# Subtracting the mean shift on VectorE instead of by TensorE products, in the last matrix of a layer's feed-forward

## The chip, the cores and the metric

The kernel runs on one core of a Trainium2 chip. The metric is the device time of one execution in microseconds (us); the time before is the median of 3 runs. The core's engines work side by side and wait for each other by semaphores: TensorE (PE in the profile, PEld for its weight loads) multiplies matrices into eight banks of accumulators (PSUM); VectorE (DVE) and ScalarE (ACT) work elementwise; GpSimd (POOL) does little here; SyncE (SP) issues transfers.

## The reference

A trunk of two layers over 256 tokens with 2048 features. Layer 0 mixes by trailing means, layer 1 by dilated attention over a shared K and V; each is followed by a gated feed-forward with a causal convolution of width 3 (inner width 5504). Every block ends in a residual with ALPHA = sqrt(2) and a layer norm:

```python
    for i in range(DEPTH):
        ...
        h = layer_norm(DEEPNORM_ALPHA * h + mix, ln1_g[i], ln1_b[i])
        ff = conv_ffn(h, ffn_w_up[i], ffn_conv_w[i], ffn_conv_b[i], ffn_w_down[i])
        h = layer_norm(DEEPNORM_ALPHA * h + ff, ln2_g[i], ln2_b[i])

def layer_norm(x, g, b):
    mu = jnp.mean(xf, axis=-1, keepdims=True)
    var = jnp.mean(jnp.square(xf - mu), axis=-1, keepdims=True)
    y = (xf - mu) * lax.rsqrt(var + LN_EPS) * g.astype(jnp.float32) + b.astype(jnp.float32)
```

The change lies in the second norm of layer 0. The result of this norm doesn't depend on a constant that is subtracted from all features of a token.

## The kernel before

**Tiling.** Features lie on partitions: the residual is four tiles `H[0]` to `H[3]` ("quarters") of 128 partitions x 4 blocks x 256 tokens. All weights are read as float32 and used as the sum of two parts: ScalarE copies a part of less precision, `wh` (L82), and VectorE takes the difference, `wl` (L83). Each matrix is worked off in units. A unit is a block of up to 512 x 512 weights: it is loaded into one of 3 buffers `raw`, split into one of 4 pairs `wh`, `wl`, and multiplied by an activation tile that is split in the same way. The list `units` sets the order on TensorE; loads run up to 5 units ahead and splits 3. The activations are `xc` (normalized), `xp` (the residual times the norm's gain, not yet normalized) or `g` (gated).

**Order.** Nothing reorders the work: each engine's instructions stand in the order in which the program issues them. A function given to `later(n, fn)` is issued after the products of the n-th unit from there, so its VectorE and ScalarE instructions stand in those queues between the splits of units ahead.

**The matrix in question.** The last three row blocks of the first feed-forward's down matrix (512, 512 and 384 rows) are multiplied by `add_last`, in four groups, one for each quarter of the output, each with four banks. The order of the units is a0 a1 b0 a2 b1 b2 c0 c1 c2 d0 d1 d2, where the letter is the quarter (0 to 3) and the digit the row block. When a group ends, `resid_last` adds its banks to the quarter (L320, L322). The rest is the layer norm:

- After quarter 0, `fold` sums its blocks; one unit later `shift` lets TensorE spread that sum over the partitions (L364), and ScalarE copies it as `cs` (L366). This is a rough mean of each token, subtracted so that the sums of squares keep their precision.
- Quarter 0 has `cs` subtracted by VectorE (L372). Quarters 1 to 3 get it on TensorE: with `shifted`, each bank's last product is followed by one with `neg1`, a constant block whose first row is -1 (L172).
- `stats` squares a quarter on ScalarE (L341) and folds it and its squares into running sums S and Q (L345, L347, L350). `xp` splits the quarter times the gain (L394, L395).
- `chain`, after the first unit of the next matrix, spreads S and Q by two products (L401, L402), works out the factor and the mean (L406 to L410), and then normalizes the quarters one by one (L415, L416, L422, L424; the lower part `xc` by L286).

The next matrix, the shared K weights, starts on `xp`, which needs no statistics (four units over 258 columns); the matrix after it, the queries', needs `xc`. In the first norm of each layer (`first`) the mix has other scalings: there VectorE does the subtraction of quarters 1 to 3 together with the factor ALPHA (L384).

Of the kernel before, what the change touches and what calls it, by code (L numbers as in the profile page):

```python
# [9 lines left out]
F32 = mybir.dt.float32  # L10
F32R = mybir.dt.float32r
I32 = mybir.dt.int32
AF = mybir.ActivationFunctionType
OP = mybir.AluOpType
# [3 lines left out]
T = 256  # L18
P = 128
# [13 lines left out]
def trunk(ctx: ExitStack, tc: tile.TileContext, x, pool_w_in, pool_w_grp, pool_scale, pool_w_out,  # L33
# [3 lines left out]
    V, A, PE = nc.vector, nc.scalar, nc.tensor  # L37
    ctx.enter_context(tc.manual_schedule())

    const = ctx.enter_context(tc.tile_pool(name="const", bufs=1))  # L40
# [7 lines left out]
    def bank(nm):  # L48
        return psp.tile([P, 512], F32, name=nm, tag="ps")
# [12 lines left out]
    def do_load(i, part=None):  # L62
        src = units[i][0]
        if src is None:
            return
        nk, n = src.shape[0] // P, src.shape[1]
        if not part:
            raw[i] = rawp.tile([P, nk, n], F32, name=f"raw{i}", tag="raw")
        rows = src.rearrange("(k p) n -> p k n", p=P)
        ks = pieces(i, nk)  # L70
        for s in ks if part is None else ks[1:] if part else ks[:1]:
            nc.sync.dma_start(raw[i][:, s], rows[:, s])
# [47 lines left out]
    def later(n, fn):  # L120
        if n == 0:
            fn()
        else:
            pending.append([n, fn])
# [22 lines left out]

    XW = T + 2

    def mm_quad(xq, ps, first, last, mode, mid, shifted):  # L150
        def go(h, l):
            nk, nb = h.shape[1], h.shape[2] // P
            order = [(k, m) for k in range(nk) for m in range(nb)]
            if last:
                order = [(k, m) for m in range(nb) for k in range(nk)]
            if first:
                for m in range(nb):
                    ps.append(bank("acc"))
            q = xq()
            n = XW if mode == "x" else T  # L160
            for i, (k, m) in enumerate(order):
                c = slice(m * P, (m + 1) * P)
                st, sp = first and k == 0, last and k == nk - 1
                if mode == "ab":
                    PE.matmul(ps[m], h[:, k, c], q[:, k, :, :T], start=st, stop=False)  # L165
                    PE.matmul(ps[m][:, :T], l[:, k, c], q[:, k, 0, :T], start=False, stop=sp and not shifted)  # L166
                else:
                    PE.matmul(ps[m][:, :n], h[:, k, c], q[:, k, 0, :n], start=st, stop=False)  # L168
                    PE.matmul(ps[m][:, :n], h[:, k, c], q[:, k, 1, :n], start=False, stop=False)  # L169
                    PE.matmul(ps[m][:, :n], l[:, k, c], q[:, k, 0, :n], start=False, stop=sp and not shifted)  # L170
                if sp and shifted:
                    PE.matmul(ps[m][:, :T], neg1, ST["cs"], start=False, stop=True)  # L172
                if mid is not None and i == 7:
                    mid()
        return go

    def group(w, r0s, c0, ncol, xqs, post, mode="ab", mids=(), shifted=False):
        ps = []
        for j, (r0, nr) in enumerate(r0s):
            last = j == len(r0s) - 1  # L180
            units.append((w[r0:r0 + nr, c0:c0 + ncol],
                          mm_quad(xqs[j], ps, j == 0, last, mode, mids[j] if j < len(mids) else None, shifted),
                          (lambda: post(ps)) if last else None))


# [110 lines left out]
    H, XC, XP, ST = {}, {}, {}, {}  # L296
    vec, cvec, gbx = [], [], {}
    ident = const.tile([P, P], F32, name="ident")
    onesd = const.tile([P, P], F32, name="onesd")
    neg1 = const.tile([P, P], F32R, name="neg1")  # L300
    ones4 = const.tile([P, P], F32R, name="ones4")
    epst = const.tile([P, 1], F32, name="epst")
    inv = const.tile([P, 1, 16], F32, name="inv")
# [9 lines left out]
    def resid_last(c, first, lay, which, after):  # L313
        def post(ps):
            for m in range(4):
                y = H[c][:, m, :]
                if first and c == 0:
                    V.scalar_tensor_tensor(y, y, ALPHA, ps[m][:, :T], op0=OP.mult, op1=OP.add)
                else:
                    V.tensor_tensor(y, y, ps[m][:, :T], OP.add)  # L320
                if c < 3:
                    V.tensor_tensor(y, y, ps[m][:, T:], OP.add)  # L322
                if c == 3 and m % 2 == 1:
                    square(3, m - 1)
            if c == 0:
                s = fold(H[0], None, "S0", F32R)
                later(1, lambda: shift(s, first, lay, which))
            elif c < 3:
                n = 3 if c == 1 and not first else 1
                later(n, lambda: stats(c))  # L330
                later(n + 1, lambda: xp(c, lay, which))
            else:
                folds(3)
                xp(3, lay, which)
                later(1, lambda: chain(ps[0], lay, which, after))
        return post
# [20 lines left out]
    def stats(q):  # L357
        square(q, 0)
        square(q, 2)
        folds(q)  # L360

    def shift(s, first, lay, which):
        ps = bank("shift")
        PE.matmul(ps[:, :T], ones4, s, start=True, stop=True)  # L364
        cs = lnp.tile([P, T], F32R, name="cs", tag="cs")
        A.copy(cs, ps[:, :T])  # L366
        ST["cs"] = cs
        cb = cs.bitcast(F32).unsqueeze(1).to_broadcast([P, 4, T])
        ST["S"] = ST["Q"] = None

        def one():
            V.tensor_tensor(H[0], H[0], cb, OP.subtract)  # L372
            if first:
                pre(1)
            stats(0)

        def two():
            xp(0, lay, which)
            if first:
                pre(2)  # L380
                pre(3)

        def pre(q):
            V.scalar_tensor_tensor(H[q], H[q], ALPHA, cb, op0=OP.mult, op1=OP.subtract)  # L384

        later(1, one)
        later(2, two)

    def xp(q, lay, which):
        g0 = 32 * which  # L390
        XP[q] = t = quad_tile("xp")
        for m in range(4):
            g = vec[lay][:, g0 + 4 * q + m:g0 + 4 * q + m + 1]
            A.activation(t[:, m, 0, :T], H[q][:, m, :], AF.Copy, scale=g)  # L394
            V.scalar_tensor_tensor(t[:, m, 1, :T], H[q][:, m, :], g, t[:, m, 0, :T].bitcast(F32),  # L395
                                   op0=OP.mult, op1=OP.subtract)
        A.copy(t[:, :, :, T:], gbx[lay, which][:, 4 * q:4 * q + 4].bitcast(F32))
# [60 lines left out]
    def add_last(w, rows, srcs, first, lay, which, after=None):  # L458
        for c in range(4):
            group(w, rows, 512 * c, 512, srcs, resid_last(c, first, lay, which, after),  # L460
                  mode="a" if c == 3 else "ab", shifted=c > 0 and not first)


    PADW = 16
# [63 lines left out]
    def add_grp(g):  # L528
# [12 lines left out]
             True, 0, 0, after=lambda q: to_tokens(q))  # L541
# [401 lines left out]
    scale = 1.0 / math.sqrt(P)  # L943
# [174 lines left out]
    with tc.tile_pool(name="start", bufs=1) as stp:  # L1118
        one1 = stp.tile([P, P], F32, name="one1")
        for q in range(NQ):  # L1120
            for t in range(2):
                XIN[q, t] = stp.tile([P, 512], F32, name=f"xin{q}{t}")
            halves = [slice(0, 256), slice(256, 512)] if q == 0 else [slice(0, 512)]
            for i, h in enumerate(halves):
                for t in range(2):
                    nc.sync.dma_start(XIN[q, t][:, h], x[0, t * P:(t + 1) * P, 512 * q:512 * q + 512][:, h])
                if q == 0:
                    do_load(0, i)
            if q in (1, 2):
                do_load(q)  # L1130
            if q < 3:
                state["loaded"] = q + 1
            if q == 0:
                make_identity(nc, ident)
                V.memset(one1, 1.0)

                warm = bank("warm")
                for i in range(WARM):
                    PE.matmul(warm[:, :P], one1, one1, start=True, stop=True)
        V.memset(onesd, 1.0 / D)  # L1140
        V.memset(neg1.bitcast(F32), 0.0)
        A.activation(neg1[0:1, :], one1[0:1, :], AF.Copy, scale=-1.0)
        A.activation(ones4, one1, AF.Copy, scale=4.0 / D)
        V.memset(epst, EPS)
        for c in range(16):
            nc.gpsimd.memset(inv[:, :, c:c + 1], 1.0 / (c + 1))
        x_quad(0, (0,))
        warm = bank("warm")
        for i in range(WARM2):
            PE.matmul(warm[:, :P], one1, one1, start=True, stop=True)  # L1150

        run_units(3)
    with tc.tile_pool(name="pool", bufs=1) as pp:
# [5 lines left out]
        for l in range(2):  # L1159
            n = 80 if l == 0 else 64  # L1160
# [95 lines left out]
```

## Time and profile before

| | |
|---|---|
| median of 3 runs | 2023.47 us (2023.33 to 2025.87) |
| the profiled execution | 2024.13 us, its span 2022.0 us |
| granted TensorE clock | 1.000 |
| the stage around the change | some 891 to 970 us from the span's start |

The span goes from the first to the last instruction; the rest lies around it. A row of a timeline gives start and duration in us, engine, line, operation, what it writes and reads, the tile, and how often; in square brackets how long the engine was idle before it and what ended that. TensorE's products overlap: one is listed with 0.28 us, while the next one starts 0.12 us later. A row of stretches gives busy time and instructions of each engine, then the granted clock (1.00 is full speed), the share of the transfer engines and their rate. A row of one line gives the shortest, median and longest duration in ns and the first and last start; rows below it name who ended its waits, with us in total and the number of times.

### The profile page before, as it was taken

What the parts mean: (1) busy time and instruction counts of PE and PEld (TensorE: products, weight loads), DVE (VectorE), ACT (ScalarE), POOL (GpSimd) and SP (SyncE); (2) the same over time, 40 slices, a digit from 0 to 9 for tenths busy, and PEclk for the clock granted to TensorE, in tenths of its full rate; (3) what the DMA queues carried; (4) which work ended last, traced back from release to release, by engine and by line L of the source; (5) the groups of instructions that cost most, each with busy time, mean ns of one, the idle gap of its engine ahead of it and who ended that gap; (6) DMA issues with size and microseconds to landing.
All of it is one profiled execution on the core that took longest, in us unless ns stands there. A gap on an engine that the chain in (4) does not pass through costs nothing.

```text
span 2022.0 us, 31645 instructions
## 1 busy us (share of the span) xinstructions
PE 2014.2 (100%) x12610; PEld 1809.2 (89%) x12610; DVE 1719.5 (85%) x2075; ACT 1270.1 (63%) x1708; POOL 111.3 (6%) x175
## 2 busy tenths in 40 slices
PE   9999999999999999999999999999999999999999
PEld 8898988899889988889898988998899989989987
DVE  6859887899789999889887878787889888989898
ACT  6544686667766686656544544487666676667672
POOL 2000000000000001100001021000001000100100
PEclk9999999999999999999999999999999999999999
DMA  8665477666666758875555656557666756666765
GB/s 259 208 205 187 164 208 211 189 190 224 215 184 192 239 178 228 219 228 179 178 194 174 214 166 205 182 187 215 184 208 190 225 186 219 198 213 194 210 214 181
DMA packets 273699, 406.73 MB, mean 201 GB/s; under 512 B 74782, under 2 KB 91060, under 8 KB 273296
## 3 DMA queue, kind: packets, MB, share of 16 engines
q1 hardware_dynamic: 259488, 388.93, 59.5%
q0 software_dynamic: 13632, 15.13, 5.0%
q8 instruction: 99, 1.62, 0.3%
q10 hardware_dynamic: 432, 0.66, 0.1%
q14 instruction: 48, 0.39, 0.1%
HBM read 380.01 MB, written 2.10 MB: 189 GB/s over the span
## 4 chain that ended last, share of the span: by engine, by line
PE 99%; DMA 0%; SPq 0%; DVE 0%; ACT 0%; issue 0%; DVEq 0%
PE acc L165 44%; PE acc L166 22%; PE s L228 3%; PE s L227 3%; PE s L229 3%; PE acc L169 3%; PE acc L170 3%; PE acc L168 3%; PE t L238 3%; PE t L240 3%; PE t L239 3%; PE t L228 2%; PE t L227 2%; PE t L229 2%; PE s L1040 0%; PE o L1093 0%
## 5 line engine op out<-in xcount | busy, mean ns | idle before, releaser
L165 PE MATMUL acc<-xc,wh 128*128 128x512 f32 x3264 | 1152.0, 396 | 0.0
L166 PE MATMUL acc<-xc,wl 128*128 128x256 f32 x3264 | 916.9, 281 | 0.0
L83 DVE TENSOR_TENSOR wl<-raw,wh 128x2048 fp32r<-128x2048 f32 (+2 forms) x313 | 676.0, 2165 | 207.8 <-ACT wh L82 206.4
L165 PEld LDWEIGHTS acc<-xc,wh 128*128 128x128 f32 x3264 | 616.2, 189 | 143.5 <-issue 0.3
L82 ACT CAST wh<-raw 128x2048 fp32r<-128x2048 f32 (+2 forms) x313 | 564.8, 1810 | 201.7 <-PE acc L165 92.2
L166 PEld LDWEIGHTS acc<-xc,wl 128*128 128x128 f32 x3264 | 615.5, 189 | 0.8 <-DVE wl L83 0.3
L96 ACT CAST wh<-raw 128x1024 fp32r<-128x1024 f32 x126 | 131.7, 1053 | 170.9 <-DVE raw L107 135.5
L97 DVE TENSOR_TENSOR wl<-raw,wh 128x1024 fp32r<-128x1024 f32 x126 | 150.4, 1221 | 3.5 <-ACT wh L96 3.5
L103 ACT CAST wh<-raw 128x1024 fp32r<-128x1024 f32 x126 | 98.7, 834 | 47.8 <-PE acc L165 24.6
L106 DVE TENSOR_TENSOR wl<-raw,wh 128x1024 fp32r<-128x1024 f32 x126 | 114.7, 951 | 4.2 <-ACT wh L103 4.0
L586 ACT ACTIVATE c<-u,cv 128x256 f32<-128x256 f32 x172 | 89.6, 593 | 19.6 <-DVE f L649 8.1
L271 POOL DMA_DIRECT2D ht<-w x24 | 20.4, 850 | 1435.3 <-DVE ht L853 388.1
L228 PE MATMUL t<-wl,g 128*128 128x256 f32 x328 | 92.3, 281 | 0.0
L227 PE MATMUL t<-wh,g 128*128 128x256 f32 x328 | 92.1, 281 | 0.0
L229 PE MATMUL t<-wh,g 128*128 128x256 f32 x328 | 91.9, 280 | 0.0
L577 ACT COPY u<-acc 128x256 f32<-128x256 f32 x164 | 53.8, 372 | 45.9 <-PE acc L166 45.9
L229 PE MATMUL s<-wh,xs 128*128 128x256 f32 x296 | 82.6, 279 | 0.0
L227 PE MATMUL s<-wh,xs 128*128 128x256 f32 x296 | 82.6, 279 | 0.0
L228 PE MATMUL s<-wl,xs 128*128 128x256 f32 x296 | 82.6, 279 | 0.0
L591 ACT ACTIVATE a<-u,cv 128x256 f32<-128x256 f32 x172 | 73.5, 499 | 12.3 <-DVE g L659 6.5
L109 DVE TENSOR_TENSOR raw<-raw 128x1024 f32<-128x1024 f32 x63 | 77.2, 1225 | 2.1
L591 ACT ACTIVATE u<-u,cv 128x256 f32<-128x256 f32 x172 | 73.5, 500 | 0.0
(337 smaller groups left out, 3540.3 us busy)
## 6 DMA issues: line engine op xcount, KB each, us to landing
raw<-in_ffn_w_up_dram SPq DMA_DIRECT2D x160, 1024.0 KB, 5.1
raw<-in_ffn_w_down_dram SPq DMA_DIRECT2D x80, 1024.0 KB, 5.2
raw<-in_pool_w_out_dram SPq DMA_DIRECT2D x16, 1024.0 KB, 5.0
raw<-in_shared_w_k_dram SPq DMA_DIRECT2D x16, 1024.0 KB, 5.3
raw<-in_attn_w_q_dram SPq DMA_DIRECT2D x16, 1024.0 KB, 5.4
raw<-in_shared_w_v_dram SPq DMA_DIRECT2D x16, 1024.0 KB, 5.3
raw<-in_attn_w_o_dram SPq DMA_DIRECT2D x16, 1024.0 KB, 5.3
raw<-in_pool_w_in_dram SPq DMA_DIRECT2D x12, 1024.0 KB, 5.6
```

The lines of the kernel that those rows point to most:

```text
L82: A.copy(wh[i][:, s], r[:, s])
L83: V.tensor_tensor(wl[i][:, s], r[:, s], wh[i][:, s].bitcast(F32), OP.subtract)
L96: A.copy(h[:, :, n], r[:, :, n])
L97: V.tensor_tensor(l[:, :, n], r[:, :, n], h[:, :, n].bitcast(F32), OP.subtract)
L103: A.copy(h[:, k, n], r[:, k, n])
L106: V.tensor_tensor(l[:, k, n], r[:, k, n], h[:, k, n].bitcast(F32), OP.subtract)
L165: PE.matmul(ps[m], h[:, k, c], q[:, k, :, :T], start=st, stop=False)
L166: PE.matmul(ps[m][:, :T], l[:, k, c], q[:, k, 0, :T], start=False, stop=sp and not shifted)
L227: PE.matmul(to, xh, h[:, k, n], start=opens and kk == 0, stop=False)
L228: PE.matmul(to, xh, l[:, k, n], start=False, stop=False)
L229: PE.matmul(to, xl, h[:, k, n], start=False, stop=ends and kk == 1)
L591: A.activation(to[:, m, :], u[:, m, i:i + T], AF.Copy, scale=cv[:, i, j:j + 1])
```

## The change

The twelve products with `neg1` go, with the constant, its fill on VectorE and the activation on ScalarE that sets its first row. In their place VectorE subtracts `cs` from quarters 1, 2 and 3 of the residual, in one instruction over 128 x 1024 each, two, three and four units after `shift`. In the first norms nothing changes.

```diff
-    def mm_quad(xq, ps, first, last, mode, mid, shifted):
+    def mm_quad(xq, ps, first, last, mode, mid):
...
-                    PE.matmul(ps[m][:, :T], l[:, k, c], q[:, k, 0, :T], start=False, stop=sp and not shifted)
+                    PE.matmul(ps[m][:, :T], l[:, k, c], q[:, k, 0, :T], start=False, stop=sp)
...
-                if sp and shifted:
-                    PE.matmul(ps[m][:, :T], neg1, ST["cs"], start=False, stop=True)
...
-    neg1 = const.tile([P, P], F32R, name="neg1")
...
+        def less(q):
+            V.tensor_tensor(H[q], H[q], cb, OP.subtract)
+
         later(1, one)
         later(2, two)
+        if not first:
+            for q in (1, 2, 3):
+                later(1 + q, lambda q=q: less(q))
...
-                  mode="a" if c == 3 else "ab", shifted=c > 0 and not first)
+                  mode="a" if c == 3 else "ab")
...
-        V.memset(neg1.bitcast(F32), 0.0)
-        A.activation(neg1[0:1, :], one1[0:1, :], AF.Copy, scale=-1.0)
```

On VectorE, between the end of quarter 1's residual and the sums of its statistics, these instructions stood before (`wl` are the weight splits of the units d0, d1 and d2, `xp` the split of quarter 0, `fold` and `S` the sums over quarter 1; the lines of the changed program have other numbers):

```order
L322 TENSOR_TENSOR h<-h,acc 128x256
L83 TENSOR_TENSOR wl_8761<-raw_8662,wh_8760 128x2048
L395 SCALAR_TENSOR_TENSOR xp<-h,vec_579,xp 128x256 x4
L83 TENSOR_TENSOR wl_8813<-raw_8704,wh_8812 128x2048
L83 TENSOR_TENSOR wl_8851<-raw_8758,wh_8850 128x1536
L345 TENSOR_TENSOR fold_8885<-h 128x512
L347 TENSOR_TENSOR S<-fold_8885 128x256
```

and these stand there now:

```order
L319 TENSOR_TENSOR h<-h,acc 128x256
L83 TENSOR_TENSOR wl_8754<-raw_8659,wh_8753 128x2048
L398 SCALAR_TENSOR_TENSOR xp<-h,vec_576,xp 128x256 x4
L384 TENSOR_TENSOR h<-h,cs 128x1024
L83 TENSOR_TENSOR wl_8807<-raw_8701,wh_8806 128x2048
L384 TENSOR_TENSOR h<-h,cs 128x1024
L83 TENSOR_TENSOR wl_8846<-raw_8751,wh_8845 128x1536
L384 TENSOR_TENSOR h<-h,cs 128x1024
L342 TENSOR_TENSOR fold_8877<-h 128x512
L344 TENSOR_TENSOR S<-fold_8877 128x256
```

The three subtractions (quarters 1, 2, 3 in this order) stand around the splits of d1 and d2; behind them the queue is the same as before. On TensorE, at the end of the last group, a product with the constant stood between the last product of the unit d2 and the first of the next matrix:

```order
L168 MATMUL acc<-g,wh_8850 128x256
L169 MATMUL acc<-g,wh_8850 128x256
L170 MATMUL acc<-g,wl_8851 128x256
L172 MATMUL acc<-cs,neg_80 128x256
L168 MATMUL acc<-xp,wh_8905 128x258
```

and now the one follows the other:

```order
L168 MATMUL acc<-g,wh_8845 128x256
L169 MATMUL acc<-g,wh_8845 128x256
L170 MATMUL acc<-g,wl_8846 128x256
L168 MATMUL acc<-xp,wh_8897 128x258
L169 MATMUL acc<-xp,wh_8897 128x258
```

So it is after each of the twelve banks of the groups b, c and d; nothing else moved on TensorE, and ScalarE, GpSimd and SyncE keep their order.

More of the change, by code (lines that the diff above doesn't have):

```diff
@@ L169, in go @@
                     PE.matmul(ps[m][:, :n], h[:, k, c], q[:, k, 1, :n], start=False, stop=False)
-                    PE.matmul(ps[m][:, :n], l[:, k, c], q[:, k, 0, :n], start=False, stop=sp and not shifted)
-                if sp and shifted:
-                    PE.matmul(ps[m][:, :T], neg1, ST["cs"], start=False, stop=True)
+                    PE.matmul(ps[m][:, :n], l[:, k, c], q[:, k, 0, :n], start=False, stop=sp)
                 if mid is not None and i == 7:
@@ L175, in mm_quad, with group @@
         return go
-    def group(w, r0s, c0, ncol, xqs, post, mode="ab", mids=(), shifted=False):
+    def group(w, r0s, c0, ncol, xqs, post, mode="ab", mids=()):
         ps = []
@@ L181, in group @@
             units.append((w[r0:r0 + nr, c0:c0 + ncol],
-                          mm_quad(xqs[j], ps, j == 0, last, mode, mids[j] if j < len(mids) else None, shifted),
+                          mm_quad(xqs[j], ps, j == 0, last, mode, mids[j] if j < len(mids) else None),
                           (lambda: post(ps)) if last else None))
```

## The prediction

> **What bounds the kernel now.** I read the page first: busy times and the chain of work that ended last.
>
> ```profile
> PE 2014.2 (100%) x12610; PEld 1809.2 (89%) x12610; DVE 1719.5 (85%) x2075; ACT 1270.1 (63%) x1708; POOL 111.3 (6%) x175
> PE 99%; DMA 0%; SPq 0%; DVE 0%; ACT 0%; issue 0%; DVEq 0%
> ```
>
> TensorE (PE) is never idle and makes the chain by itself. So a product taken away is time gained, as long as nothing else makes PE wait; a wait put in front of PE anywhere is time lost, because no later PE idle time is there to absorb it. The average share of VectorE (DVE), 85%, says nothing of the place that changes, so next I read the busy times around it in stretches of 10 us.
>
> ```profile
> core 0: us, PE busy (x) PEld busy (x) DVE busy (x) ACT busy (x) POOL busy (x), PEclk, DMA share, GB/s
> 910.00:920.00 10.00, 10.00 (x84) 9.86 (x83) 9.72 (x20) 7.86 (x13) 0.00 (x0) 1.00 0.48 165
> 920.00:930.00 10.00, 10.00 (x86) 10.00 (x85) 9.86 (x16) 2.83 (x5) 0.00 (x0) 1.00 0.61 210
> ```
>
> Here VectorE is as full as TensorE (9.72 and 9.86 of 10 us). The third look is whether TensorE already waits for it, at the mean products that close this matrix's layer norm (L401, L402):
>
> ```profile
> L402 PE MATMUL acc<-Q,onesd x2: 379/422/466, 933.4 to 933.7; 128*128 128x256 f32 x2
>   DVE Q L350: 0.2, 1
> L402 PE MATMUL acc<-Q,onesd x2: 378/379/380, 223.0 to 223.3; 128*128 128x256 f32 x2
> 931.42 0.43 DVE L350 TENSOR_TENSOR S<-S 128x256 f32<-128x256 f32 x1
> 932.94 0.43 DVE L350 TENSOR_TENSOR Q<-Q 128x256 f32<-128x256 f32 x1
> 933.00 0.60 PE L401 MATMUL acc<-S,onesd 128*128 128x256 f32 x2
> 933.43 0.68 PE L402 MATMUL acc<-Q,onesd 128*128 128x256 f32 x2
> ```
>
> It does. Q is ready at 932.94 + 0.43 = 933.37, L402 comes at 933.43, and one of its two passes takes 466 ns where the same line takes 379 in the first layer norm (the third row, at 223): PE waits for VectorE's Q already, for about 0.1 us. The two engines reach this place together, so the place has no slack on VectorE's side, and this decides the sign.
>
> **What is removed.** Twelve products and their weight loads on TensorE.
>
> ```profile
> L172 PE MATMUL acc<-cs,neg x12: 277/280/283, 891.6 to 927.1; 128*128 128x256 f32 x12
> 927.02 0.28 PE L170 MATMUL acc<-g,wl 128*128 128x256 f32 x1
> 927.14 0.28 PE L172 MATMUL acc<-cs,neg 128*128 128x256 f32 x1
> 927.25 0.28 PE L168 MATMUL acc<-xp,wh 128*128 128x258 f32 x1
> ```
>
> The 280 ns of one overlap with its neighbours. What it costs PE is its pitch, start to start: 927.25 - 927.14 = 0.11, 927.14 - 927.02 = 0.12. I take 0.118, so 12 x 0.118 = 1.4 us, all of it ahead of L401: PE would get there at 933.00 - 1.4 = 931.6. Bounds: 12 x 0.11 = 1.3 and 12 x 0.12 = 1.45. At the program's start a fill on VectorE and one small activation go too:
>
> ```profile
> 2.03 0.31 ACT L1142 ACTIVATE neg<-one 1x128 fp32r<-1x128 f32 x1
> 4.80 0.58 ACT L521 CAST xc<-xT 128x512 fp32r<-128x512 f32 x1 [2.26 <-PE xT L518]
> ```
>
> ScalarE (ACT) then idles 2.26 us for a transpose, so these 0.3 us give nothing; without that cover it would be 0.3.
>
> **What is added.** Three subtractions over 128x1024 on VectorE. The form stands in the trace: L372 does the same to quarter 0.
>
> ```profile
> L366 ACT CAST cs<-shift x1: 372/372/372, 890.8 to 890.8; 128x256 fp32r<-128x256 f32 x1
> L372 DVE TENSOR_TENSOR h<-h,cs x1: 1218/1218/1218, 894.2 to 894.2; 128x1024 f32<-128x1024 f32 x1
> 949.91 1.22 DVE L286 TENSOR_TENSOR xc<-h,xc 128x1024 fp32r<-128x1024 f32 x1
> 951.05 1.22 DVE L415 TENSOR_TENSOR h<-h,rm 128x1024 f32<-128x1024 f32 x1
> 952.30 1.23 DVE L416 TENSOR_TENSOR h<-h,rm 128x1024 f32<-128x1024 f32 x1
> ```
>
> Each is busy for 1.22 us and takes 951.05 - 949.91 = 1.14 us of the queue when the next instruction doesn't need its result, 952.30 - 951.05 = 1.25 when it does. In the new order an independent instruction follows each of the three, so 3 x 1.14 = 3.42 us; the upper bound is 3 x 1.25 = 3.75. Their inputs are no wait: the shift was copied at 890.8, and quarter 3 is the last to be brought back to features:
>
> ```profile
> L803 SPq DMA_DIRECT2D h<-hb x16: 585/609/611, 864.6 to 878.8; - x16
> DMA to landing us min/median/max: 2.0/4.2/5.8
> ```
>
> The last issue, at 878.8 + 0.6, lands by 885.2 at the latest, and its subtraction comes 25 us later.
>
> **What of it VectorE can absorb.** These are the rows between which the three are put:
>
> ```profile
> 900.94 2.28 DVE L83 TENSOR_TENSOR wl<-raw,wh 128x2048 fp32r<-128x2048 f32 x1
> 903.14 1.67 DVE L395 SCALAR_TENSOR_TENSOR xp<-h,vec,xp 128x256 fp32r<-128x256 f32 x4
> 904.73 2.29 DVE L83 TENSOR_TENSOR wl<-raw,wh 128x2048 fp32r<-128x2048 f32 x1
> 906.60 1.48 ACT L82 CAST wh<-raw 128x1536 fp32r<-128x1536 f32 x1 [3.70 <-PE acc L165]
> 908.12 1.76 DVE L83 TENSOR_TENSOR wl<-raw,wh 128x1536 fp32r<-128x1536 f32 x1 [1.10 <-ACT wh L82]
> 909.79 0.69 DVE L345 TENSOR_TENSOR fold<-h 128x512 f32<-128x512 f32 x1
> DVE wl L83 <- ACT wh L82: 1.1, 1, 1.1
> DVE rm L409 <- ACT rm L408: 0.6, 1, 0.6
> ```
>
> I walk the queue. The subtraction of quarter 1 starts at 904.73. The split behind it starts at 905.87 and keeps its pitch (903.14 - 900.94 = 2.20) to 908.07; then quarter 2, to 909.21. The short split that before stood idle 1.10 us for ScalarE now finds its input ready (that cast ends at 906.60 + 1.48 = 908.08) and runs its 909.79 - 908.12 = 1.67 to 910.88; quarter 3 ends the insert at 912.02. There the fold of quarter 1 follows, which started at 909.79: VectorE is 2.23 us late. Of the 3.42 us, 1.19 went into the one hole.
>
> The last two rows are all waits of VectorE between 909.7 and 945. After the hole there is none until L409, which lies behind L402. So the 2.23 us reach S and Q undiminished: S at 931.42 + 0.43 + 2.23 = 934.1, Q at 933.37 + 2.23 = 935.6.
>
> **What the wait does.** PE is at L401 at 931.6 and waits until 934.1, about 2.5 us; it does L401 (933.43 - 933.00 = 0.43) and waits for Q from 934.5 to 935.6, about 1.1 us more. It leaves L402 2.23 us later than before: the 1.4 us saved are waited away, and 2.2 us on top. In the instruction order the rest of the next matrix stands behind L402 on PE, so all of it is late, with the other engines that feed it. What is due next is the split input of the following matrix:
>
> ```profile
> 951.28 0.48 PE L165 MATMUL acc<-xc,wh 128*128 128x512 f32 x1
> 951.59 0.28 PE L166 MATMUL acc<-xc,wl 128*128 128x256 f32 x1
> 951.71 0.39 PE L165 MATMUL acc<-xc,wh 128*128 128x512 f32 x1
> 951.94 0.28 PE L166 MATMUL acc<-xc,wl 128*128 128x256 f32 x1
> 915.98 2.29 DVE L83 TENSOR_TENSOR wl<-raw,wh 128x2048 fp32r<-128x2048 f32 x1
> ```
>
> L286 has it ready at 949.91 + 1.22 = 951.13, PE takes it at 951.28, and the step of 951.59 - 951.28 = 0.31 where later ones take 0.23 (951.94 - 951.71) shows that this meeting is tight as well. VectorE is 2.2 us late there and so is PE: nothing is added and nothing recovered. The weight splits are not hit: the one for the unit that starts at 927.25 is the last row, done at 915.98 + 2.29 = 918.3, so 2.2 us leave it over 5 us, even with PE 1.4 us early.
>
> Sum: -1.4 + 3.6 of wait = +2.2 us, from 2.2 (1.14 each) to 2.6 (1.25 each); with the hole wider, since PE frees ScalarE's buffer some 0.5 us early, the cast comes earlier and nothing changes, as VectorE gets there only at 909.2. I take +2.2. The profiled execution took 2024.13 us (its span, 2022.0, and 2.1 around it) and becomes 2026.3. It is 0.66 above the median of the runs shown, 2023.47, so the median becomes 2025.7.
>
> One rule speaks against even this. The Trainium skill, page "TensorE: Matmul & The Clock Gate", section "Why this matters for your kernels", says to leave no idle gap of more than about 3 us on PE, or its clock falls to half. The trace's nearest gap is shorter:
>
> ```profile
> 10.24 0.39 PE L168 MATMUL acc<-xc,wh 128*128 128x256 f32 x1 [2.03 <-ACT wh L82]
> 8.00:12.00 4.00, 1.75 (x12) 1.33 (x11) 1.90 (x4) 1.86 (x3) 0.00 (x0) 1.00 0.96 332
> ```
>
> After 2.03 us of idle PE the granted clock stays 1.00, with PE busy for 1.75 of those 4 us. The new wait is 2.5 + 1.1 us with 0.43 us of work between, longer than any here, so the rows don't exclude a fall. By the rows alone the sum stays +2.2; the fall is a rival below. By the limit that the Trainium skill gives, neither piece is long enough by itself, and both together would be.
>
> **Rivals.** (1) VectorE's work stays hidden and PE keeps its 1.4 us: 2023.47 - 1.4 = 2022.1. It needs 2.2 us of slack at Q, against a wait of 0.1 us that is there already; for it speaks only that PE's records are modelled at their ends. (2) The lateness is larger: the three take 1.25 each and the hole absorbs nothing, because ScalarE's cast moves with it: 3 x 1.25 = 3.75, so 2027.2. Against it: on ScalarE that cast stands ahead of the first instruction that needs a subtracted quarter. (3) The other side of the line, **slower by a clear amount**: the broken wait at L401 and L402 lowers PE's granted clock. At half clock the pitch goes from 0.12 to 0.24, so a low stretch as long as the wait (3.6 us) costs 1.8 us more, 2027.5, and one twice as long 3.6 more, 2029.3. It decides as soon as the clock falls at all, since VectorE's next due times move along and PE has no slack to make it good.
>
> **How the numbers follow.** About 0.2%, 4 us, is what a measurement of this kernel can tell from no change; the three runs alone lie 2.5 us apart. Forecast of +2.2: chance 0.54, its own range 2024.5 to 2027.3; since half the limit is used up, 0.16 of this measures as slower. (1) 0.10, of which 0.04 measures as faster. (2) 0.15, at 3.75 of 4.05 us, 0.09 of it over the limit. (3) 0.21, all slower. Slower is 0.16 + 0.09 + 0.21 = 0.46, faster 0.04, within 0.50. The time is the likeliest case's, 2025.7; the range goes from case (1) at 2022.0 to the middle of case (3), 2028.6.
>
> **What would show it.** VectorE's hole of 1.10 us at 908 is gone, the fold of quarter 1 starts near 912.0, and Q ends near 935.6 (absolute times move with the run's start by little). TensorE, which had no wait here, shows one of some 2.5 us for S and 1.1 us for Q at these two lines, and the unit behind them begins 2.2 us later than before and keeps that distance to the end. A granted clock below 1.00 between 930 and 950 would be case (3). No wait at these lines, or Q earlier than 934, would refute the walk; a wait of the right size with the end not moved would mean that PE has slack later, which the chain of waits denies.

## The result and the profile after

| | before | changed |
|---|---|---|
| median, 12 runs each | 2025.12 us (2023.33 to 2026.64) | 2028.81 us (2025.89 to 2031.13) |
| ratio | 1 | 1.002, 95% interval 1.0013 to 1.0027 |
| profiled execution (span) | 2024.13 us (2022.0) | 2025.89 us (2024.1) |
| mean granted clock of the runs | 1.000 in the profiled one | 0.997 to 0.999 in all twelve |

The changed kernel is slower by 0.2%, 2.6 to 5.5 us by the interval. That is more than the 2.2 us that were forecast, and the median lies 0.2 us above the range. With all twelve runs of the kernel before, its own median is 1.65 us higher than that of the three runs that the forecast started from.

First the waits of TensorE between 900 and 1240 us of the changed kernel (who waited for whom: us in total, times, longest). The kernel before had none of this size there.

```profile
PE acc L404 <- DVE S L347: 2.2, 1, 2.2
PE acc L405 <- DVE Q L347: 0.4, 1, 0.4
```

Both are at the mean products of this norm (L401 and L402 before, L404 and L405 now). Next VectorE's timeline in the changed kernel, around the three subtractions and at the end of S and Q:

```profile
903.67 1.22 DVE L384 TENSOR_TENSOR h<-h,cs 128x1024 f32<-128x1024 f32 x1
904.81 2.28 DVE L83 TENSOR_TENSOR wl<-raw,wh 128x2048 fp32r<-128x2048 f32 x1
907.01 1.22 DVE L384 TENSOR_TENSOR h<-h,cs 128x1024 f32<-128x1024 f32 x1
908.15 1.75 DVE L83 TENSOR_TENSOR wl<-raw,wh 128x1536 fp32r<-128x1536 f32 x1
909.82 1.22 DVE L384 TENSOR_TENSOR h<-h,cs 128x1024 f32<-128x1024 f32 x1
910.95 0.68 DVE L342 TENSOR_TENSOR fold<-h 128x512 f32<-128x512 f32 x1
...
932.59 0.42 DVE L347 TENSOR_TENSOR S<-S 128x256 f32<-128x256 f32 x1
...
934.11 0.42 DVE L347 TENSOR_TENSOR Q<-Q 128x256 f32<-128x256 f32 x1
```

This execution stands 1.12 us earlier ahead of the change (the product that spreads quarter 0's sum comes at 889.32, before at 890.44; both are quoted below). With 1.12 added the fold of quarter 1 starts at 912.07 and Q ends at 935.65; the walk gave 912.02 and 935.6. The hole of 1.10 us is gone, and each subtraction takes 1.14 us of the queue. What the walk doesn't show is on TensorE, in its timeline and in stretches of 2 us of the same kernel (the number behind the busy times is the granted clock):

```profile
930.55 0.28 PE L170 MATMUL acc<-xp,wl 128*128 128x258 f32 x1
933.07 1.14 PE L404 MATMUL acc<-S,onesd 128*128 128x256 f32 x2 [2.24 <-DVE S L347]
934.59 1.22 PE L405 MATMUL acc<-Q,onesd 128*128 128x256 f32 x2 [0.38 <-DVE Q L347]
935.25 0.78 PE L168 MATMUL acc<-xp,wh 128*128 128x258 f32 x1
935.82 0.42 PE L169 MATMUL acc<-xp,wh 128*128 128x258 f32 x1
936.04 0.42 PE L170 MATMUL acc<-xp,wl 128*128 128x258 f32 x1
936.25 0.42 PE L168 MATMUL acc<-xp,wh 128*128 128x258 f32 x1
936.47 0.35 PE L169 MATMUL acc<-xp,wh 128*128 128x258 f32 x1
936.65 0.28 PE L170 MATMUL acc<-xp,wl 128*128 128x258 f32 x1
936.77 0.29 PE L168 MATMUL acc<-xp,wh 128*128 128x258 f32 x1
```
```profile
930.00:932.00 2.00, 0.83 (x7) 0.62 (x6) 1.97 (x6) 1.20 (x3) 0.00 (x0) 1.00 0.63 179
932.00:934.00 2.00, 0.93 (x2) 0.42 (x2) 1.90 (x5) 2.00 (x7) 0.00 (x0) 0.80 1.02 393
934.00:936.00 2.00, 1.62 (x5) 1.23 (x5) 1.97 (x6) 1.68 (x2) 0.00 (x0) 0.50 0.23 86
936.00:938.00 2.00, 2.00 (x17) 2.00 (x16) 2.00 (x2) 1.52 (x2) 0.00 (x0) 0.85 0.00 0
```

The clock falls to 0.50 as the wait for S ends: a mean of 0.80 from 932 to 934 is 0.8 us at 0.50, so it fell near 933.2. Products that come 0.12 us apart come 0.21 to 0.22 us apart from 935.82 to 936.47, and from 936.65 on 0.12 again. L404 itself takes 1.14 us for its two passes (0.60 before), so little of the wait for Q is left to be seen as idle time.

To measure the stage alone, free of what runs differ by elsewhere, I take two instructions that every version has: the product that spreads quarter 0's sum in this norm and the same product in the first norm of layer 1. Here they are in the kernel before, then in the changed one:

```profile
890.44 0.28 PE L364 MATMUL shift<-S,ones 128*128 128x256 f32 x1
1243.52 0.28 PE L364 MATMUL shift<-S,ones 128*128 128x256 f32 x1
```
```profile
889.32 0.34 PE L361 MATMUL shift<-S,ones 128*128 128x256 f32 x1
1245.30 0.28 PE L361 MATMUL shift<-S,ones 128*128 128x256 f32 x1
```

The distance is 353.08 us before and 355.98 now: +2.90 us, of which the walk has 2.23. From here on "stage" means this distance less 353.08; it comes from one profile of each version, and the medians and ratios come from all its runs, set against the kernel before on the same chip. Two runs, one of `e4_both` (4164.90 us) and one of the kernel before on the chip of `e5_split2` (2162.48 us), stand far above all others and are not in the ratios.

### The profile page after: what moved, and what is told of

It reads as the page before. It is cut to its first block, busy times and chain, and to the rows that moved or that the text cites. A ratio compares the mean times of both kernels' runs of the same rounds, so it can differ in the third digit from the quotient of the medians.

```text
span 2024.1 us, 31623 instructions
## 1 busy us (share of the span) xinstructions
PE 2014.4 (100%) x12598; PEld 1808.0 (89%) x12598; DVE 1722.7 (85%) x2077; ACT 1271.2 (63%) x1707; POOL 111.6 (6%) x175
## 4 chain that ended last, share of the span: by engine, by line
PE 98%; DVE 1%; DMA 1%; SPq 0%; issue 0%; ACT 0%; DVEq 0%
PE acc L165 43%; PE acc L166 22%; PE s L226 3%; PE s L225 3%; PE s L227 3%; PE t L236 3%; PE t L238 3%; PE t L237 3%; PE acc L169 3%; PE acc L170 3%; PE acc L168 3%; PE t L226 2%; PE t L225 2%; PE t L227 2%; DVE wl L83 0%; PE s L1043 0%
```

## The experiments

Theory A: VectorE's queue alone sets when TensorE leaves the two mean products. Theory B: the twelve products are worth their 1.4 us, and the subtractions cost more than that. The clock is a part beside either.

**Neither products nor subtractions** (`e1_none`):

```diff
-        if not first:
-            for q in (1, 2, 3):
-                later(1 + q, lambda q=q: less(q))
```

> The changed kernel without its three subtractions and without the products: quarters 1 to 3 keep the mean shift, so this leaves out part of the computation. Theory A (VectorE's queue alone sets when TensorE leaves the mean products, so TensorE's 1.4 us are worth nothing): TensorE comes 1.4 us early and waits for S and Q by about 1.4 us in sum; Q as late as before; time within 0.5 us of the kernel before. Theory B (the products' 1.4 us are gained, the subtractions cost more than that by themselves): 1.4 us or more below the kernel before, no new wait.

Measured: ratio 1.0 (0.9991 to 1.0009); stage -0.43. Theory B's gain of 1.4 us isn't there, and TensorE waits for Q again. The waits in this version, of TensorE and of VectorE:

```profile
PE acc L402 <- DVE Q L347: 0.7, 1, 0.7
```
```profile
DVE wl L83 <- ACT wh L82: 0.7, 1, 0.7
DVE rm L409 <- ACT rm L408: 0.6, 1, 0.6
```

The wait for Q is shorter than the 1.4 us expected. The second fence has the reason for 0.4 us of that: VectorE's hole is 0.7 us where it was 1.1. With four products less by then, TensorE frees ScalarE's weight buffer earlier, the cast ends earlier, and VectorE gains 0.4 us. So the products are worth 0.4 us, by way of VectorE's queue.

**One subtraction, eight products** (`e2_one`; on the kernel before):

```diff
+        if not first:
+            later(2, lambda: less(1))
...
-                  mode="a" if c == 3 else "ab", shifted=c > 0 and not first)
+                  mode="a" if c == 3 else "ab", shifted=c > 1 and not first)
```

> Quarter 1 by VectorE, quarters 2 and 3 by eight products. Theory A: 1.14 us of VectorE's queue fit into its 1.19 us hole at 907 us, so Q is not late; TensorE comes 0.5 us early and waits 0.5 to 0.6 us for Q; time within 0.5 us of the kernel before, granted clock 1.00. Theory B: a third of the way to the changed kernel, +1.0 to +1.3 us.

Measured: ratio 1.0002 (0.9993 to 1.001); stage -0.06. The wait for Q shows as 0.2 us of idle time, less than the 0.5 to 0.6 expected. Set against the kernel before, TensorE comes there 0.44 us early and leaves 0.08 us early, so it loses 0.36 us. The hole takes one subtraction at no cost.

**Two subtractions, four products** (`e8_two`, the same with `less` for quarters 1 and 2 and `c > 2`):

> Quarters 1 and 2 by VectorE, quarter 3 by four products: the dose between one (0) and three (+2.2 us). Theory A: 2 x 1.14 - 1.19 = 1.09 us late at Q, TensorE 0.94 us early, two waits of about 0.9 and 1.1 us; +1.1 us, no fall of the clock, as after the waits of 0.95 and 0.82 us with all products kept. A cost in proportion to the subtractions: two thirds of the changed kernel, +2.5 us.

Measured: ratio 1.0008 (0.9999 to 1.0017); stage +1.11. The dose is a hole and then a straight line: -0.06, +1.11, and +2.23 for three with the clock kept (next). TensorE's timeline of this version, at S and Q:

```profile
931.94 0.70 PE L407 MATMUL acc<-S,onesd 128*128 128x256 f32 x2 [0.70 <-DVE S L350]
933.46 0.70 PE L408 MATMUL acc<-Q,onesd 128*128 128x256 f32 x2 [0.82 <-DVE Q L350]
933.80 0.47 PE L168 MATMUL acc<-xp,wh 128*128 128x258 f32 x1
```

Two pieces of idle time under 1 us, both pairs of passes at the usual pace: the clock stayed at 1.00 from 930 to 940.

**The wait filled with work** (`e3_warm`, run a second time as `e3_again`). On the changed kernel, products that nobody reads:

```diff
+        def fill(n):
+            if (lay, which) == (0, 1):
+                for i in range(n):
+                    PE.matmul(ps[:, T:], ones4, ST["cs"], start=True, stop=True)
+
+        fill(20)
         PE.matmul(ps[:, :T], onesd, ST["S"], start=True, stop=True)
+        fill(9)
```

> The changed kernel, with 20 products whose results nobody reads in front of the product of S and 9 in front of that of Q, so that TensorE works where it waited. Theory A with a clock part (the gap of 2.2 us on TensorE lowers its granted clock for 3.4 us or more, and this is what goes beyond +2.2 us): granted clock 1.00 between 930 and 940 us, +2.2 us against the kernel before, and runs closer together than the changed kernel's (2025.9 to 2031.1). Rival (lateness alone, the rest of the difference is spread of runs): time and spread as the changed kernel's, about +3.7 us.

Measured: ratio 1.0011 (1.0002 to 1.002); stage +2.23, the walk's number. Its TensorE timeline has no idle time and the usual pace behind it:

```profile
931.53 2.55 PE L407 MATMUL acc<-cs,ones 128*128 128x256 f32 x20
933.95 0.70 PE L410 MATMUL acc<-S,onesd 128*128 128x256 f32 x2
934.29 1.42 PE L407 MATMUL acc<-cs,ones 128*128 128x256 f32 x9
935.56 0.61 PE L412 MATMUL acc<-Q,onesd 128*128 128x256 f32 x2
935.81 0.47 PE L168 MATMUL acc<-xp,wh 128*128 128x258 f32 x1
936.12 0.29 PE L169 MATMUL acc<-xp,wh 128*128 128x258 f32 x1
936.25 0.28 PE L170 MATMUL acc<-xp,wl 128*128 128x258 f32 x1
```

The changed kernel hadn't run beside it on one chip, so both ran again together:

> The changed kernel again, beside the filled one on the same chip, to compare the two directly. With the clock part: mean granted clock under 1.00 in nearly all runs, +3.0 to +4.5 us against the kernel before. If the first measurement was high by chance: +2.2 us, as the filled one.

> The filled version again: +2.2 us against the kernel before, 1 us or more under the changed kernel though it issues 29 products more; clock 1.00 in two thirds of the runs, as the kernel before has it.

Measured on that chip: the changed kernel 2028.07 us, ratio 1.0017 (1.0009 to 1.0026), clock under 1.00 in 9 of 11 runs; the filled one 2025.50 us, ratio 1.0007 (0.9998 to 1.0016), under 1.00 in 1 of 11. Twenty-nine products more make it 2.6 us faster by the medians. The stage is +4.15 and +2.25 (the filled version's first profile: +2.23). The second profile of the changed kernel shows a longer fall; its stretches:

```profile
932.00:934.00 2.00, 0.93 (x2) 0.50 (x2) 1.90 (x5) 2.00 (x7) 0.00 (x0) 0.70 1.02 395
934.00:936.00 2.00, 1.70 (x5) 1.23 (x5) 1.97 (x6) 1.68 (x2) 0.00 (x0) 0.50 0.24 91
936.00:938.00 2.00, 2.00 (x12) 2.00 (x11) 2.00 (x2) 1.52 (x2) 0.00 (x0) 0.50 0.00 0
938.00:940.00 2.00, 2.00 (x12) 2.00 (x12) 1.43 (x3) 1.31 (x2) 0.00 (x0) 0.60 0.31 20
940.00:942.00 2.00, 2.00 (x19) 2.00 (x18) 1.97 (x3) 0.99 (x1) 0.00 (x0) 1.00 0.94 360
```

Twelve products in 2 us where nineteen are usual (one that reaches over an edge counts on both sides). A mean of 0.70 with a low value of 0.50 is 1.2 us of low clock in that stretch; with 2, 2 and 1.6 us (for 0.60) it is 6.8 us. The same sum for the first profile is 0.8 + 2 + 0.6 = 3.4 us. So the clock is low until 936.6 (933.2 + 3.4) and 939.6 (932.8 + 6.8). What counts is the low time after TensorE has started the product of Q, at 934.59 in both profiles. In the kernel before, that product came at 933.43 and the next one here:

```profile
933.77 0.47 PE L168 MATMUL acc<-xp,wh 128*128 128x258 f32 x1
```

That is 0.34 us; at half clock it is 935.25 - 934.59 = 0.66. Behind it products come 0.215 us apart for 0.12, so 0.44 of the time from 935.25 on is lost: 0.6 and 1.9 us. In all the clock costs 0.9 and 2.2 us there. The stage is beyond 2.23 by less, 0.67 and 1.92 us, because some 0.3 us come back at the query matrix. In the kernel before, TensorE met VectorE at the first split input of that matrix (the rows at 951.28 and 951.59, 0.31 apart). In the changed kernel TensorE is later than VectorE there, and the step is 0.23:

```profile
953.36 0.39 PE L165 MATMUL acc<-xc,wh 128*128 128x512 f32 x1
953.59 0.28 PE L166 MATMUL acc<-xc,wl 128*128 128x256 f32 x1
```

The two inputs behind it do the same. Over the three TensorE's lateness goes from 3.22 to 2.91 us in this profile and from 4.48 to 4.17 in the other.

**Subtractions and products both** (`e4_both`: the kernel before with all three calls of `less`):

> The kernel before with the three subtractions added and its twelve products kept: the mean is taken from quarters 1 to 3 twice. Theory A: VectorE is late by 2.2 us as in the changed kernel, TensorE comes to S 1.4 us later than there and waits about 1.1 us for S and 1.1 us for Q; +2.2 us against the kernel before, with the granted clock at 1.00 if a gap of 1.1 us is too short for a fall, so 1 to 2 us less than the changed kernel although it does more work. Theory B: 1.4 us more than the changed kernel, +5 us.

Measured: ratio 1.0011 (1.0002 to 1.002); stage +2.29. TensorE's timeline at S and Q, with the waits that were expected at 1.1 us each:

```profile
934.83 0.70 PE L407 MATMUL acc<-S,onesd 128*128 128x256 f32 x2 [0.95 <-DVE S L350]
936.35 0.70 PE L408 MATMUL acc<-Q,onesd 128*128 128x256 f32 x2 [0.82 <-DVE Q L350]
936.70 0.47 PE L168 MATMUL acc<-xp,wh 128*128 128x258 f32 x1
```

The granted clock is 1.00 from 924 to 946 us. With the products kept, VectorE's work costs the same 2.2 us, against 2.90 and 4.15 for the changed kernel without them, by the profiles; the two versions didn't run on one chip. So taking the products out did harm: it made the gap on TensorE longer, and the clock fell. Theory B, at +5, is out. (This profile also has TensorE waiting 1.4 us for quarter 0's sum, ahead of the stage. ScalarE had waited 5.11 us for a weight transfer before 864.6, against 3.50 in the kernel before; that this is the cause isn't shown.)

**One weight split less ahead of Q** (`e5_split2` on the changed kernel, `e9_two_split2` on the version with two subtractions, `e7_before_split2` on the kernel before):

```diff
+        if marks[1] - 3 <= i < marks[1] + 8:
+            n = 2
         while state["split"] < min(len(units), i + n + 1):
```

> The changed kernel, with the weight splits of the units from the last group to the end of the query matrix made two units ahead and not three, so that one split (2.20 us of VectorE) leaves the queue ahead of Q and goes behind the norm. Theory A: VectorE is late by 2.23 - 2.20 = 0.03 us, Q stands where it stood before the change, TensorE still comes 1.4 us early and waits: within 0.5 us of the kernel before, about 2.2 us and the clock part under the changed kernel. If the lateness did not come from VectorE's queue: as the changed kernel, +3.7 us.

> Two subtractions by VectorE, four products, and one split less ahead of Q: Q 1.1 us earlier than before the change, TensorE 0.94 us earlier, so no wait at S and Q, and the eight products are gained: 0.9 to 1.1 us under the kernel before between the two mean products of the norms at 890 and 1244 us. If TensorE's products are worth nothing whatever VectorE does: as the kernel before.

> The kernel before with the splits two units ahead there, the control to the two above: TensorE is the bound and only its small waits go (0.1 us at Q, 0.08 us three times at the split inputs of the query matrix): 0.1 to 0.4 us under the kernel before. If the split distance itself is worth more: as far under it as the version with two subtractions.

Measured: `e5_split2` ratio 1.0003 (0.9994 to 1.0012), stage +1.17; `e9_two_split2` 1.0002 (0.9993 to 1.0011), stage +0.08; `e7_before_split2` 1.0001 (0.9992 to 1.001), stage -0.38. The first two miss by about 0.9 us, and their waits show where: a new one, at the first value unit, whose split now stood on ScalarE behind the reading of the key banks. TensorE's wait in `e9_two_split2`:

```profile
PE t L241 <- DVE wl L83: 0.9, 1, 0.9
```

The wait costs more than its idle time: from the product ahead of it to the second one behind it, both versions lose 1.2 us against the kernel before. Less that they stand at 0.0 and -1.1, as expected; S and Q are no longer waited for in `e9_two_split2`.

The same profile shows a low clock at another place, the program's start. TensorE's gap there, and the stretches around and behind it:

```profile
9.63 0.39 PE L170 MATMUL acc<-xc,wh 128*128 128x256 f32 x1 [1.60 <-ACT wh L82]
8.00:12.00 4.00, 2.17 (x15) 1.94 (x15) 2.04 (x3) 1.86 (x3) 0.00 (x0) 0.95 0.98 327
12.00:16.00 4.00, 4.00 (x25) 4.00 (x24) 2.44 (x4) 2.95 (x6) 0.00 (x0) 0.63 1.05 398
```

The kernel before, in the second of these stretches:

```profile
12.00:16.00 4.00, 4.00 (x36) 4.00 (x35) 2.74 (x6) 3.09 (x7) 0.00 (x0) 1.00 1.02 372
```

The means give 0.4 + 3.0 = 3.4 us at 0.50, from 11.6 on, behind a gap of 1.60 us. In the kernel before, the gap at this place was longer, 2.03 us, and the clock stayed at 1.00. So the length of a gap alone doesn't decide, and one profile without a fall doesn't show that a gap of that length is safe.

`e10_order` puts that one split back ahead of the key banks:

```diff
         later(5, lambda: lo(3))
+
+        def one_split():
+            do_split(state["split"])
+            state["split"] += 1
+
+        if (lay, which) == (0, 1):
+            later(5, one_split)
```

> Two subtractions, four products, splits two units ahead, and the split of the first value unit put back ahead of the reading of the key banks, where the last version made TensorE wait 0.9 us. Theory A: no wait of TensorE from 930 to 1240 us, 0.7 to 1.1 us under the kernel before between the two mean products of the norms at 890 and 1244 us; in the whole time too little to tell from no change. If another wait comes in its place: within 0.3 us of the kernel before.

Measured: stage -0.93, no wait of TensorE between 890 and 1240 us, clock 1.00 in all 11 runs; median 2023.18 against 2023.91 us, ratio 0.9996 (0.9987 to 1.0005). In the stage it beats both kernels, and by 0.55 us the control `e7_before_split2`; in the whole time it can't be told from the kernel before.

## Why the prediction was wrong

**What held.** TensorE is the bound and keeps nearly all that is put in front of it. At Q the two engines arrive together, so the products' 1.4 us are not gained: without them and without the subtractions the stage gains 0.43, through the cast and the hole. (The sum rightly gave that way nothing in the changed kernel, where VectorE gets to that split later.) One subtraction goes into the hole, and each further one costs its 1.14 us. The walk's +2.23 is what the stage shows with the clock kept (2.23 and 2.25), and VectorE's times are right within 0.05 us. The wait for S (2.24 against 2.5) is right too; that for Q (0.38 against 1.1) is shorter because L404, at half clock, filled part of it.

**The step that failed** is the decision under the sum: "By the rows alone the sum stays +2.2; the fall is a rival below." It put the clock at nothing in the sum. The fall was no rival but the rule: 21 of the 23 runs of the changed kernel have a mean clock under 1.00 (3.4 us at 0.50 make 0.999 of such a run), against 4 of 22 with the wait filled. In the two runs that were profiled it stands at these products. So the case that got a chance of 0.21 is the usual one. The nearest row, 2.03 us of idle time without a fall at the program's start, was too weak to carry that decision: 1.60 us at the same place is followed by a fall in another profile. The mechanism of rival (3) is right, and its price of 1.8 to 3.6 us too high, since 1.4 and 1.8 us of the low time lie ahead of the product of Q, for which TensorE had to wait in any case: 0.9 and 2.2 us at the place, 0.67 and 1.92 in the stage. Added to 2.23 these give 2.90 and 4.15 us, and the 3.7 us between the medians lies between them.

A smaller thing is wrong too: "nothing is added and nothing recovered" at the split input of the query matrix. Once the clock has made TensorE the later of the two, 0.3 us come back there.

The median lies above the range for two reasons: this clock part, and three first runs of the kernel before that gave a median 1.65 us under that of all twelve. (The range's upper end is called the middle of case (3); from 2027.5 and 2029.3 that is 2028.4, not 2028.6.)

The Trainium skill, page "TensorE: Matmul & The Clock Gate", Part 1 on the clock gate, says that the clock halves after at least one idle window of about 3.4 us, that the window runs free of the program, and that it takes a busy window to come back. The halving agrees (0.50), and so do the stretches, 3.4 and 6.8 us, one window and two. The length of the gap does not: 2.24 and 2.26 us of idle time were enough here, and 1.60 us came ahead of a fall in `e9_two_split2`. That the window runs free fits the moments: the fall came 0.1 us after the gap's end in the first profile (933.2 against 933.07), 0.3 us before it in the second (932.8) and 2 us after it at the program's start (11.6 against 9.63). That its place decides whether the clock falls, and for one window or two, is only argued; no run here shows it.

**What stays open.** The clock is under 1.00 also in a quarter to a third of the runs of the kernel before (9 of 33, 10 of 32 and 9 of 27 on three chips), at some 2 us each by the medians of the two kinds. Its profiled execution has none of it, so where it falls there wasn't seen; the start of the program, where `e9_two_split2` has it, is a candidate. That the two short gaps leave the clock alone rests on one profile each of `e8_two` and `e4_both`; over their runs it is under 1.00 in 5 of 11 and 5 of 10.

## What to carry to other kernels

Where two engines arrive at a place together, work moved from one to the other is not a trade: what is taken off the first isn't gained, and what is put on the second is paid, less the holes of its queue. Price a new wait on TensorE twice, once as lateness and once as lost clock, and don't take one profile without a fall for a limit. At this place two gaps of under 1 us, 1.8 us in sum, cost nothing beyond themselves, and one of 2.24 us with 0.38 behind it cost up to 2 us more; whether the longest gap or the sum counts, the runs don't separate. If a wait can't be removed, work that nobody needs in front of it can be worth it.

## What the runs showed of the hardware

- With a gap of 2.24 us on TensorE the granted clock went to 0.50 for 3.4 us in one profile, with one of 2.26 us for 6.8 us in another. Gaps of 0.70 and 0.82, and of 0.95 and 0.82 us, left it at 1.00 in one profile each.
- At the program's start a gap of 1.60 us was followed by 3.4 us at 0.50 in one profile, and one of 2.03 us by none in another.
- At half clock the products of 258 columns come 0.21 to 0.22 us apart, against 0.12.
- 29 products in the gap (2.55 and 1.42 us by their rows) made the kernel 2.6 us faster by the medians of one chip; the stage went from +4.15 to +2.25.
